# A weave of two matmul streams made eight units longer, with six transposes moved into it

## The chip, the cores and the metric

The kernel runs on one core of a Trainium2 chip. The metric is the device time of one execution in microseconds. The median of three runs before the change is 2181.49 us (2178.9 to 2183.92). The profile is of one more execution, of 2180.43 us.

## The reference

One layer of a streaming encoder on 256 rows of 2048 columns, all in 32-bit floating point. What matters here is the middle part, the mixer, with two branches whose results are merged by gates:

```
proj = x @ w_in                      # q, k, v, o of the mLSTM; sq, sk, sv; gates ga, gb
y_m  = head_norm(mlstm(q, k, v)) * sigmoid(o)          # 256 x 1024
y_sb = stick_breaking(sq, sk, sv)                      # 256 x 1024
merged = sigmoid(ga) * (y_m @ w_up_m) + sigmoid(gb) * (y_sb @ w_up_sb)   # 256 x 2048
x = layer_norm(ALPHA * x + merged @ w_out)
```

Ahead of it and behind it stands a SwiGLU network of 5632 hidden columns with a layer norm, and at the end an embedding that is added through a gate.

## The kernel before

**Units.** All large products run as units. A unit is one tile of weights (256 rows by up to 512 columns) against one half (128 rows, `t` = 0 or 1) of the activations. Both sides are split in two parts, a rounded one (`hi`) and the rest (`lo`), so a unit is six matmuls (lines 1286 to 1288): hi by hi, hi by lo and lo by hi, for two blocks of 128 rows. A tile of weights comes by DMA from the SP queue (line 1207) as a raw page; ScalarE makes the `hi` part (line 1235) and VectorE the `lo` part (line 1239), in `split_one`. How many raw pages and split tiles are held ahead is given by the mode: `HELD` has (5, 6) for "mix", (6, 6) for "woven" and (8, 6) for "wide".

**Two kinds of streams.** `group` makes plain units: each tile is used for `t` = 0 and `t` = 1, and the two results grow in two PSUM accumulators. `both7` makes two blocks of columns with seven products instead of eight: 28 units, each with a tile of its own, after sums of weights on VectorE (line 361) and of accumulators (lines 397 and 403). Products 1 and 2 have one accumulator each at a time; products 5, 7, 6, 4 and 3 are interleaved and have five open together. When the seven are closed, `in_two` plans the two sigmoids of a pair of results `DELAY["sig"]` = 5.0 us later (line 240 by way of `activate`).

**The weave.** `weave(main, side)` puts the units of `side` between those of `main`, in proportion to columns: after each main unit as many side units as keep the two at the same fraction. In the mixer, `main` is the mLSTM values `v`, the stick-breaking columns `sb`, the two gates of group 0 (`branch`) and the up groups `ups(0)`, `ups(1)`, `ups(2)`: 176 units, sixteen of them of half width, so 168 in whole columns. An up group `g` is eight units with `w_up_m` on `ymT` (the mLSTM half) and eight with `w_up_sb` on `ysbT`. `side` is five `both7` of 28 units: values of the stick-breaking heads, output gates, and `pair(1)`, `pair(2)`, `pair(3)`, the two gates of groups 1 to 3. After the weave come the mode "mix", `bring_back`, which fetches the four parked blocks of the residual rows (line 272), then `ups(3)` and the product with `w_out`.

**The end of an up group.** `up_done(g, half)` runs when an accumulator is complete. It has the planner go on (`sched.until`) until the gate's sigmoid for this half is emitted, then VectorE multiplies the accumulator with the gate (line 1047) and, at the second half, adds the two halves (line 1049). `merge_turn(g, t)` turns the merged 128 x 512 block for the `w_out` product: `transposed` takes a PSUM bank, TensorE transposes four blocks (line 290), ScalarE casts (line 292), VectorE subtracts (line 297). For group 3 it is spawned `DELAY["mt"]` = 3.2 us after the addition; for groups 0 to 2 in one entry of the program behind the weave.

**What sets the order.** The order of instructions on every engine is the order in which this Python program emits them. Each entry of `program` is a unit, a mode or a function. A planner (`Sched`) has a clock that a whole unit moves on by 6 x 0.2161 us; generators are spawned with a delay and run when the clock has passed it. The instructions that they emit stand in each engine's queue at that place. After each unit `splits_due` emits splits, and with them additions of line 361, until six split tiles are held. PSUM has one pool of eight banks (`PSUM_BUFS`), which accumulators and transposes share, and SBUF one pool of 48 pages; a tile that takes a freed bank or page waits for the last access to it.

```
def misc(shape):
    return ps_pool.tile(shape, F32, name="ms", tag="ps")
...
        if u.start:
            u.acc["ps"] = ps_pool.tile([P, COL], F32, name="mm", tag="ps")
```

Of the kernel before, what the change touches and what calls it, by code (L numbers as in the profile page):

```python
# [15 lines left out]
TT = S // P  # L16
# [160 lines left out]
def flat(pairs):  # L177
    return [u for p in pairs for u in p]
# [7 lines left out]
def kernel(  # L186
# [19 lines left out]
    sched = Sched()  # L206
# [19 lines left out]
    def act_tile():  # L226
        return page_pool.tile([P, 2, 4, P], F32R, name="actT", tag="page")
# [59 lines left out]
    def transposed(src, act, c, t):  # L287
        ps = misc([P, 4, P])
        for k in range(4):
            nc.tensor.transpose(ps[:, k], src[:, k * P:(k + 1) * P], ident[:])  # L290
        dst = act.get(c, t)
        nc.scalar.copy(dst[:, 0], ps[:])  # L292
        if act.soon:
            if c not in act.whole:
                act.whole[c] = big()
            nc.scalar.copy(act.whole[c][:, t * COL:(t + 1) * COL], ps.rearrange("q k s -> q (k s)"))  # L296
        nc.vector.tensor_tensor(out=dst[:, 1], in0=ps[:], in1=dst[:, 0], op=ALU.subtract)  # L297
        act.mark(c, t, 4)
        if act.soon and all(act.ready(c, h) for h in range(TT)):
            sched.spawn(form_turn(act, c), DELAY["form"] + 5.0 * c)  # L300
# [35 lines left out]
    def group(w, rows, col0, cols, act, done):  # L336

        accs = [{} for _ in range(TT)]
        pairs = []
        for i, r in enumerate(rows):  # L340
            tile = plain(rows_of(w, r, col0, cols))
            pairs.append([Unit(tile, t, accs[t], act, r // COL, r % COL // P,
                               i == 0, i == len(rows) - 1, done) for t in range(TT)])
        return pairs
# [88 lines left out]
    program = []  # L433

    def mode(name):
        program.append(Mode(name))
# [252 lines left out]
    def sb_columns(ps, t, heads):  # L689

        n = len(heads) * DS
        stage = temp()
        nc.scalar.copy(stage[:, :n], ps[:, :n])
        sched.spaced(sb_turn(t, stage, heads), DELAY["sbt"], BANK_GAP)
# [110 lines left out]
    def v_done(g):  # L805
        def done(ps, t):
            st["v", t, g] = big()[:, 0:2 * (DM + 1)].rearrange("q (h d) -> q h d", d=DM + 1)
            nc.scalar.copy(st["v", t, g][:, :, DM:], ones[:, 0:2].rearrange("q (h d) -> q h d", d=1))
            nc.scalar.copy(st["v", t, g][:, :, 0:DM], ps.rearrange("q (h d) -> q h d", d=DM))
            flags.add(("v", t, g))  # L810
        return done
# [38 lines left out]
    def ym_rows(c, t):  # L850
        r = (c * TT + t) * P
        return ym_away[r:r + P, :].rearrange("p (k a q) -> p k a q", k=2, a=4)
# [6 lines left out]
    def bring_ym_back(units):  # L859

        def one(c, t):
            ymT.tiles[c, t] = act_tile()
            nc.sync.dma_start(out=ymT.tiles[c, t][:].bitcast(F32), in_=ym_rows(c, t))

        out = []
        for i in range(0, len(units), 4):
            out += [lambda i=i: one(i // 8, i // 4 % 2)] + units[i:i + 4] if i < 16 else units[i:i + 4]
        return out
# [58 lines left out]
    def gated(h):  # L927

        yield from wait(("hs", h), ("mo", 0, h // 2), ("mo", 1, h // 2))
        due = max(sched.now, st.get("gated", 0.0))  # L930
        st["gated"] = due + GATED_GAP
        yield due - sched.now
        hs = st["hs", h // 2][:, h % 2]
        for t in range(TT):
            nc.vector.tensor_tensor(out=hs[:, t], in0=hs[:, t], in1=st["mo", t][:, h * DM:(h + 1) * DM], op=ALU.mult)
        yield bank(DELAY["m4"])
        ps = misc([P, TT, 2, P])
        parts = []
        for t in range(TT):
            for b in range(2):  # L940
                nc.tensor.transpose(ps[:, t, b], hs[:, t, b * P:(b + 1) * P], ident[:])
                k = 2 * (h % 2) + b
                parts.append((ymT.get(h // 2, t)[:, :, k], ps[:, t, b], hs[:, t, b * P:(b + 1) * P],
                              st["cw"][:, 64 + 2 * h + b:65 + 2 * h + b]))
        for _, src, y, g in parts:
            activate(y, src, ACT.Copy, scale=g)
        for d, _, y, _ in parts:
            nc.scalar.copy(d[:, 0], y)
            nc.vector.tensor_tensor(out=d[:, 1], in0=y, in1=d[:, 0], op=ALU.subtract)
        for t in range(TT):  # L950
            ymT.mark(h // 2, t, 2)
            if ymT.ready(h // 2, t):
                sched.spawn(put_ym_away(h // 2, t), DELAY["away"])
# [44 lines left out]
    def in_sequence(gens):  # L998
        for g in gens:
            yield from g  # L1000
# [10 lines left out]
    def v(g):  # L1011
        return flat(group(w_in, range(0, D, 2 * P), 2048 + g * COL, COL, x1T, v_done(g)))

    def sb(*heads):
        col0 = [(sq0 + h * DS, 2 * DS) for h in heads[::2]]
        return flat(group(w_in, range(0, D, 2 * P), col0, len(heads) * DS, x1T,
                          lambda ps, t: sb_columns(ps, t, heads)))
# [4 lines left out]
    def lane():  # L1022

        for h in heads:
            yield from stick(h)
# [6 lines left out]
    def gate_done(g, half):  # L1032
        def done(ps, t):
            if (g, t) not in gt:
                gt[g, t] = big()
            activate(gt[g, t][:, half * COL:(half + 1) * COL], ps, ACT.Sigmoid)
            flags.add(("gate", g, t, half))
        return done

    def merged(g, t):  # L1040
        return gt[g // 2 * 2, t][:, g % 2 * COL:(g % 2 + 1) * COL]

    def up_done(g, half, last):
        def done(ps, t):
            sched.until(lambda: ("gate", g, t, half) in flags)
            a = gt[g, t][:, half * COL:(half + 1) * COL]
            nc.vector.tensor_tensor(out=a, in0=ps, in1=a, op=ALU.mult)  # L1047
            if last:
                nc.vector.tensor_tensor(out=merged(g, t), in0=gt[g, t][:, 0:COL], in1=gt[g, t][:, COL:], op=ALU.add)
                if g == 3:  # L1050
                    sched.spawn(merge_turn(g, t), DELAY["mt"])
        return done

    def merge_turn(g, t):
        transposed(merged(g, t), mergedT, g, t)
        return
        yield

    def branch(g, half):
        return flat(group(w_in, range(0, D, 2 * P), ga0 + half * D + g * COL, COL, x1T, gate_done(g, half)))  # L1060

    def ups(g, swap=False):
        parts = [flat(group(w_up_m, range(0, HM * DM, 2 * P), g * COL, COL, ymT, up_done(g, 0, swap))),
                 flat(group(w_up_sb, range(0, HS * DS, 2 * P), g * COL, COL, ysbT, up_done(g, 1, not swap)))]
        if swap:
            parts.reverse()
        return parts[0] + parts[1]
# [10 lines left out]

    program.append(lambda: [sched.spawn(lane()) for _ in range(2)])
    program.append(lambda: sched.spawn(in_sequence([gated(h) for h in range(HM)])))  # L1080
    gate = branch(0, 1)
    main = v(0) + v(1) + sb(8, 9, 2, 3) + sb(10, 11, 4, 5) + [Mode("wide")] + sb(12, 13, 6, 7) + sb(14, 15) + [lambda: sched.spawn(lane())] + branch(0, 0) + gate[:4] + bring_ym_back(gate[4:] + ups(0)) + ups(1) + ups(2)
    mode("woven")
    program.extend(weave(main, both7(w_in, sq0 + 2 * HS * DS, sq0 + 2 * HS * DS + COL, x1T, sv_dest, sv_ready, 0)
                         + both7(w_in, 3072, 3072 + COL, x1T, mo_dest, mo_ready, 0) + pair(1) + pair(2) + pair(3)))
    mode("mix")
    program.append(bring_back)
    program.append(lambda: [sched.spawn(merge_turn(g, t), 1.0 + 2.0 * g + t) for g in range(3) for t in range(TT)])
    program.extend(ups(3))

    x2T = ActT(act_tile, ActT(act_tile))
    norm2 = Norm(ln2_g[0], ln2_b[0], x2T, ALPHA, (4.0, 1.0))
# [175 lines left out]
    for u in program:  # L1268
# [14 lines left out]
        for k in range(2):  # L1283
            hi, lo = a[:, 0, u.sub + k], a[:, 1, u.sub + k]
            first, last = u.start and k == 0, u.stop and k == 1
# [38 lines left out]
```

## Time and profile before

| | us |
|---|---|
| median of three runs (lowest, highest) | 2181.49 (2178.9, 2183.92) |
| the profiled execution's own time | 2180.43 |
| its span, first to last instruction | 2178.7 |
| TensorE busy with matmuls | 2170.4 |
| VectorE busy | 1936.1 |
| ScalarE busy | 1325.9 |
| first unit of the weave starts at | 806.16 |
| first unit behind the weave starts at | 1268.0 |

The span runs from the first to the last instruction; the execution's own time is 1.7 us longer. PE is TensorE's matmuls, PEld its loading of the stationary operand, DVE VectorE, ACT ScalarE, POOL GpSimd, SP the queue that issues nearly all DMAs. Matmuls overlap in the pipeline: one of 512 columns lasts about 0.39 us, but the next one starts 0.23 us after it, so time per unit is read from starts, and a busy TensorE says only that no gap was seen. The granted clock of TensorE is 1.00 in every stretch. In a row of a timeline stand start, duration, engine, line, operation, output and inputs, and in brackets the idle time of the engine before it with what ended it.

### The profile page before, as it was taken

To read this page: it belongs to the slowest core of one execution; us is meant where nothing else is said; L and a number is where in the kernel's file an instruction comes from. 1 tells how busy PE (TensorE), PEld (TensorE's weight loads), DVE (VectorE), ACT (ScalarE), POOL (GpSimd) and SP (SyncE) were. 2 spreads that over 40 slices of the span, in tenths; PEclk is the share of its full clock that TensorE was granted. 3 is DMA by queue.
4 is the path that set the end of the run, shared out by engine and by line. 5 is a ranking of instruction groups with operands and counts; after the bars stand their busy time and mean duration, and the time that the engine had idled before them with its cause. 6 is when DMAs were issued, how large, how long until landed. Compare 5 with 4: busy or idle time off the path is not lost.

```text
span 2178.7 us, 28297 instructions
## 1 busy us (share of the span) xinstructions
PE 2170.4 (100%) x9942; PEld 1796.9 (82%) x9942; DVE 1936.1 (89%) x2131; ACT 1325.9 (61%) x1632; POOL 97.9 (4%) x88
## 2 busy tenths in 40 slices
PE   9999999999999999999999999999999999999999
PEld 7888888888888888888888888888888888888888
DVE  6899999999998789898989985799999999999974
ACT  7565655556564766667766564565665555665572
POOL 0100000010000000000000000000010000000000
PEclk9999999999999999999999999999999999999999
DMA  9899999999995676776878876589999999999753
GB/s 328 254 300 287 288 291 309 282 278 314 313 326 174 212 229 210 224 232 202 281 233 270 283 263 211 183 235 312 286 279 302 296 284 291 311 297 319 259 165 101
DMA packets 304399, 572.72 MB, mean 263 GB/s; under 512 B 18392, under 2 KB 39808, under 8 KB 304256
## 3 DMA queue, kind: packets, MB, share of 16 engines
q1 hardware_dynamic: 282496, 528.96, 72.8%
q0 software_dynamic: 21760, 41.95, 11.2%
q8 instruction: 78, 1.28, 0.2%
q14 instruction: 65, 0.53, 0.1%
HBM read 564.55 MB, written 6.29 MB: 262 GB/s over the span
## 4 chain that ended last, share of the span: by engine, by line
PE 96%; DVE 2%; issue 1%; ACT 1%; DMA 0%; SPq 0%; DVEq 0%
PE mm L1286 31%; PE mm L1288 31%; PE mm L1287 31%; PE ms L290 1%; DVE split L1239 1%; DVE raw L361 1%; PE ms L496 0%; PE ms L987 0%; PE ms L885 0%; PE ms L963 0%; PE ms L900 0%; PE ms L976 0%; DVE temp L796 0%; ACT split L1235 0%; DMA big<-in_x_dram 0%
## 5 line engine op out<-in xcount | busy, mean ns | idle before, releaser
L1235 ACT CAST split<-raw 128x1024 fp32r<-128x1024 f32 (+2 forms) x1073 | 1072.5, 1038 | 535.6 <-PE mm L1287 170.9
L1239 DVE TENSOR_TENSOR split<-raw,split 128x1024 fp32r<-128x1024 f32 (+2 forms) x1073 | 1255.5, 1201 | 111.6 <-ACT split L1235 99.2
L1286 PE MATMUL mm<-split,actT 128*128 128x512 f32 (+2 forms) x3112 | 1214.0, 390 | 0.7 <-ACT big L240 0.4
L1288 PE MATMUL mm<-split,actT 128*128 128x512 f32 (+2 forms) x3112 | 1200.0, 386 | 0.6 <-DVE actT L297 0.6
L1287 PE MATMUL mm<-split,actT 128*128 128x512 f32 (+2 forms) x3112 | 1199.1, 385 | 0.4 <-DVE split L1239 0.3
L1288 PEld LDWEIGHTS mm<-split,actT 128*128 128x128 f32 x3112 | 584.7, 188 | 120.6 <-DVE actT L297 1.4
L1286 PEld LDWEIGHTS mm<-split,actT 128*128 128x128 f32 x3112 | 585.2, 188 | 115.9 <-DVE big L1047 1.2
L1287 PEld LDWEIGHTS mm<-split,actT 128*128 128x128 f32 x3112 | 585.5, 188 | 115.4 <-DVE split L1239 3.2
L361 DVE TENSOR_TENSOR raw<-raw 128x1024 f32<-128x1024 f32 x256 | 312.0, 1219 | 2.3
L1212 POOL DMA_DIRECT2D raw<-in_ffn_w_dram x80 | 95.5, 1193 | 1872.8 <-DMA raw<-in_ffn_w_dram 1150.8
L292 ACT CAST actT<-ms 128x512 fp32r<-128x512 f32 x60 | 35.1, 586 | 85.5 <-PE ms L290 84.8
L569 DVE TENSOR_TENSOR temp<-mm,temp 128x512 f32<-128x512 f32 x112 | 76.8, 685 | 3.5 <-PE mm L1288 1.2
L622 DVE SCALAR_TENSOR_TENSOR big<-mm,big 128x512 f32<-128x512 f32 x96 | 65.3, 682 | 3.5 <-PE mm L1288 3.5
L297 DVE TENSOR_TENSOR actT<-ms,actT 128x512 fp32r<-128x512 f32 x60 | 40.8, 684 | 19.3 <-ACT big L296 10.5
L285 DVE TENSOR_TENSOR actT<-temp,actT 128x512 fp32r<-128x512 f32 x40 | 26.5, 687 | 17.4 <-ACT actT L284 17.3
L236 ACT ACT_TABLE_LOAD x31 | 39.8, 1283 | 0.5
L240 ACT ACTIVATE temp<-mm 128x512 f32<-128x512 f32 (+1 forms) x22 | 12.3, 560 | 45.2 <-PE mm L1288 45.2
L240 ACT ACTIVATE temp<-temp 128x512 f32<-128x512 f32 (+1 forms) x48 | 28.6, 595 | 6.7 <-DVE temp L569 6.6
L284 ACT CAST actT<-temp 128x512 fp32r<-128x512 f32 x40 | 24.1, 621 | 13.0 <-DVE temp L308 12.0
L1098 DVE SCALAR_TENSOR_TENSOR big<-big,mm 128x512 f32<-128x512 f32 x8 | 5.5, 685 | 25.3 <-PE mm L1288 25.3
L240 ACT ACTIVATE temp<-ms,gbT 128x128 f32<-128x128 f32 x64 | 24.1, 460 | 5.6 <-PE ms L496 5.6
L1152 DVE TENSOR_TENSOR temp<-temp,big 128x512 f32<-128x512 f32 (+1 forms) x10 | 5.8, 582 | 23.7 <-ACT temp L240 23.7
(131 smaller groups left out, 562.5 us busy)
## 6 DMA issues: line engine op xcount, KB each, us to landing
raw<-in_ffn_w_dram SPq DMA_DIRECT2D x655, 512.0 KB, 6.0
raw<-in_w_in_dram SPq DMA_DIRECT2D x184, 512.0 KB, 4.6
raw<-in_ffn_w_dram POOLq DMA_DIRECT2D x80, 512.0 KB, 8.7
raw<-in_w_out_dram SPq DMA_DIRECT2D x32, 512.0 KB, 6.1
raw<-in_w_in_dram SPq DMA_DIRECT2D x56, 256.0 KB, 3.8
raw<-in_w_ple_gate_dram SPq DMA_DIRECT2D x24, 512.0 KB, 5.5
raw<-in_w_up_m_dram SPq DMA_DIRECT2D x16, 512.0 KB, 5.1
raw<-in_w_up_sb_dram SPq DMA_DIRECT2D x16, 512.0 KB, 5.5
```

What stands on the lines that cost most here:

```text
L236: nc.scalar.preload_act_table_set(table[0])
L240: nc.scalar.activation(out, in_, func, **kw)
L297: nc.vector.tensor_tensor(out=dst[:, 1], in0=ps[:], in1=dst[:, 0], op=ALU.subtract)
L361: nc.vector.tensor_tensor(out=out.tile[:, :, :cols], in0=a.tile[:, :, :cols], in1=b.tile[:, :, :cols], op=ALU.add)
L569: nc.vector.tensor_tensor(out=out, in0=a, in1=b, op=op)
L622: nc.vector.scalar_tensor_tensor(out=xs, in0=ps, scalar=0.5, in1=xs, op0=ALU.mult, op1=ALU.add)
L1212: nc.gpsimd.dma_start(out=r.tile[:, :, :r.cols], in_=r.plus[0], accum_op=ALU.add)
L1235: nc.scalar.copy(hi[:, ks], r[:, ks])
L1239: nc.vector.tensor_tensor(out=lo[:, ks], in0=r[:, ks], in1=hi[:, ks], op=ALU.subtract)
L1286: nc.tensor.matmul(ps, hi, w[0][:, k, :u.cols], start=first, stop=False)
L1287: nc.tensor.matmul(ps, hi, w[1][:, k, :u.cols], start=False, stop=False)
L1288: nc.tensor.matmul(ps, lo, w[0][:, k, :u.cols], start=False, stop=last)
```

## The change

`ups(3)` is made ahead of the weave and cut in two. Its first eight units (the mLSTM half) are appended to `main`, so the weave has 184 main units, 176 in whole columns, with the same 140 side units. Its second eight units stay behind the weave, after the mode "mix" and `bring_back`. The six `merge_turn` of groups 0 to 2 are spawned by a new entry `merge_turns` in `main`, between `ups(2)` and the eight units; their delays are 1, 4, 7, 10, 13 and 16 us instead of 1, 2, 3, 4, 5 and 6.

```diff
+    def merge_turns():
+        for g in range(3):
+            for t in range(TT):
+                sched.spawn(merge_turn(g, t), 1.0 + 3.0 * (2 * g + t))
+
+    gate, last = branch(0, 1), ups(3)
-    gate = branch(0, 1)
-    main = v(0) + v(1) + sb(8, 9, 2, 3) + sb(10, 11, 4, 5) + [Mode("wide")] + sb(12, 13, 6, 7) + sb(14, 15) + [lambda: sched.spawn(lane())] + branch(0, 0) + gate[:4] + bring_ym_back(gate[4:] + ups(0)) + ups(1) + ups(2)
+    main = v(0) + v(1) + sb(8, 9, 2, 3) + sb(10, 11, 4, 5) + [Mode("wide")] + sb(12, 13, 6, 7) + sb(14, 15) + [lambda: sched.spawn(lane())] + branch(0, 0) + gate[:4] + bring_ym_back(gate[4:] + ups(0)) + ups(1) + ups(2) + [merge_turns] + last[:8]
     mode("woven")
...
     mode("mix")
     program.append(bring_back)
-    program.append(lambda: [sched.spawn(merge_turn(g, t), 1.0 + 2.0 * g + t) for g in range(3) for t in range(TT)])
-    program.extend(ups(3))
+    program.extend(last[8:])
```

## The prediction

> **What bounds the kernel now.** I read the head of the page first, then the chain of waits, then a table of busy time by stage from the start of the weave, and last the engines' own timelines around the place of the edit.
>
> ```profile
> span 2178.7 us, 28297 instructions
> PE 2170.4 (100%) x9942; PEld 1796.9 (82%) x9942; DVE 1936.1 (89%) x2131; ACT 1325.9 (61%) x1632; POOL 97.9 (4%) x88
> PE 96%; DVE 2%; issue 1%; ACT 1%; DMA 0%; SPq 0%; DVEq 0%
> ```
>
> TensorE is never idle for long: 2178.7 - 2170.4 = 8.3 us in the whole span, and 96% of the chain that ended last is its matmuls. The edit takes no matmul and no transpose away. So it can win only time in which TensorE waits, and only near the place of the edit. The table by stage has that (columns: stretch, its length, busy time of PE, PEld, DVE, ACT, POOL, granted clock, DMA share, GB/s):
>
> ```profile
> 806.16:842.00 35.84, 35.54 (x161) 29.08 (x160) 33.72 (x46) 21.89 (x28) 0.00 (x0) 1.00 0.63 181
> 842.00:900.00 58.00, 57.87 (x255) 46.34 (x254) 55.26 (x64) 39.90 (x56) 0.00 (x0) 1.00 0.76 235
> ...
> 1100.00:1200.00 100.00, 99.28 (x441) 81.19 (x440) 87.50 (x93) 65.82 (x79) 0.00 (x0) 1.00 0.79 248
> 1200.00:1225.32 25.32, 25.32 (x114) 20.96 (x112) 25.25 (x24) 14.35 (x14) 0.00 (x0) 1.00 0.87 275
> 1225.32:1251.54 26.22, 26.03 (x114) 20.94 (x112) 26.12 (x27) 14.68 (x15) 0.00 (x0) 1.00 0.90 289
> 1251.54:1268.00 16.46, 16.46 (x73) 13.62 (x73) 16.39 (x17) 10.34 (x13) 0.00 (x0) 1.00 0.67 217
> 1268.00:1288.00 20.00, 20.00 (x101) 16.66 (x100) 19.93 (x25) 12.90 (x17) 0.00 (x0) 1.00 0.87 298
> 1288.00:1314.00 26.00, 26.00 (x120) 21.52 (x119) 13.60 (x15) 14.67 (x16) 0.00 (x0) 1.00 0.78 248
> sum 507.84, PE 506.47 PEld 416.80 DVE 458.17 ACT 338.81 POOL 0.00; mean PE 50.65 PEld 41.68 DVE 45.82 ACT 33.88 POOL 0.00
> ```
>
> The stretch 806.16 to 1268.00 is the weave, found by counting units of six matmuls in TensorE's order. Over it and the 46 us behind it TensorE idles 507.84 - 506.47 = 1.37 us. That is the whole stock of visible waits that the edit can reach. VectorE tells the other half: from 1200 to 1288 it is busy 87.69 of 88.00 us. It is full there, TensorE is just held. From 1288 on it has slack (13.60 of 26 us). Where VectorE does hold TensorE is seen in the waits of 1200 to 1315 and in the chain:
>
> ```profile
> PEld mm L1286 <- DVE big L1047: 0.6, 1, 0.6
> PEld mm L1287 <- DVE split L1239: 0.3, 1, 0.3
> ...
> 1250.89 0.61 DVE big L1047
> 1251.54 0.50 PE mm L1286
> ```
>
> At 1251.54 the first matmul of a new accumulator waits until VectorE has emptied an older one (line 1047): there is no free PSUM bank. The pool has eight (`PSUM_BUFS`); late in a pair of columns `both7` keeps five accumulators open, the up group two, and when one half group follows another two more are asked for.
>
> **The change part by part.** A unit takes 1.36 us, a group of four transposes about 0.47 us more than none, and a split on VectorE 1.15 us back to back:
>
> ```profile
> 1279.63 0.39 PE L1286 MATMUL mm<-split,actT 128*128 128x512 f32 x1
> 1280.99 0.39 PE L1286 MATMUL mm<-split,actT 128*128 128x512 f32 x1
> 1277.10 0.60 PE L290 MATMUL ms<-ident,big 128*128 128x128 f32 x4
> 1278.93 0.40 PE L1286 MATMUL mm<-split,actT 128*128 128x512 f32 x1
> 1256.54 6.89 DVE L1239 TENSOR_TENSOR split<-raw,split 128x1024 fp32r<-128x1024 f32 x6
> ```
>
> (1280.99 - 1279.63 = 1.36; 1278.93 - 1277.10 = 1.83 holds four transposes and one unit, so 0.47; 6.89 / 6 = 1.15.)
>
> *Eight units move into the weave.* Matmuls are the same in number: 0 on TensorE. What moves is VectorE's share. The main list grows from 168 to 176 units (in whole columns), so per main unit 140 / 176 = 0.80 side units follow instead of 0.83. A side unit costs VectorE one split and on average 16/28 of an addition (line 361, as long as a split), 1.15 x 1.57 = 1.81 us for 1.36 us of TensorE: 0.45 us too much. The eight moved units cost it four splits and two multiplications (line 1047, 0.68 us), 6.0 us for 10.9 us of TensorE: 4.9 us of VectorE's time come back inside the weave. The gain on the path is between 0 and the 1.37 us above; the waits lie at several places (806 to 842 has 0.30, 1100 to 1200 has 0.72, 1225 to 1251 has 0.19) and only the last and part of the rest feel a density that falls by 4.5%. I take 0.4 us.
>
> *Six merges move into the weave and apart.* Each is four transposes, a cast on ScalarE (line 292) and a subtraction on VectorE (line 297). TensorE's part is the same as before, six times 0.47 us; before, two of them stood together (0.89 instead of 0.94), so +0.05 us. What is new is where their PSUM bank comes from. Before, they came when all side accumulators were closed. Now five side banks and two up banks are open, so one bank is left, and each merge waits until VectorE has done the one before it. How long that takes, the six of before show:
>
> ```profile
> 1269.36 0.60 PE L290 MATMUL ms<-ident,big 128*128 128x128 f32 x4
> 1271.18 0.60 PE L290 MATMUL ms<-ident,big 128*128 128x128 f32 x4
> 1273.02 0.60 PE L290 MATMUL ms<-ident,big 128*128 128x128 f32 x4
> 1274.85 1.03 PE L290 MATMUL ms<-ident,big 128*128 128x128 f32 x8
> 1275.52 1.28 DVE L297 TENSOR_TENSOR actT<-ms,actT 128x512 fp32r<-128x512 f32 x2
> 1277.85 1.88 DVE L297 TENSOR_TENSOR actT<-ms,actT 128x512 fp32r<-128x512 f32 x3
> 1280.78 0.68 DVE L297 TENSOR_TENSOR actT<-ms,actT 128x512 fp32r<-128x512 f32 x1
> 1295.28 0.60 PE L290 MATMUL ms<-ident,big 128*128 128x128 f32 x4
> 1296.53 0.69 DVE L297 TENSOR_TENSOR actT<-ms,actT 128x512 fp32r<-128x512 f32 x1 [1.23 <-ACT actT L292]
> 1263.36 1.41 DVE L397 TENSOR_TENSOR big<-mm,big 128x512 f32<-128x512 f32 x2
> ```
>
> From the first transpose to the end of the subtraction: 1276.2 - 1269.36 = 6.8 us, then 5.6, 5.5, 4.3, 4.4, and 4.4 for the last (1277.10 to 1281.46); where VectorE was idle, 1.9 us (1295.28 to 1297.22). Before, nobody waited for these banks. In the change, writing out the order by the weave's rule and the planner's clock (1.297 us a unit), the merges follow after main unit 169, then 3, 2, 2 and 3 units later; the sixth is forced one unit later by the gate's wait below. In time: 3 x 1.36 + 0.47 = 4.5 us, or 2 x 1.36 + 0.47 = 3.2 us. Against turns of 6.8, 5.6 and 5.5 the second, third and fourth would wait 2.3, 2.4 and 2.3 us, 7.0 us in sum, if VectorE stayed as far behind as before. Two things speak for less. Each us that TensorE waits, VectorE catches up, so the waits don't add up: the sum tends to the largest, 2.4 us. And at the merges' start VectorE is less far behind: the side stands at 134 of 140, so six side units (6 x 0.45 = 2.7 us) and the closing sums of `both7` (lines 397 and 403, six of 0.68 us, 4.1 us) are backlog not yet made, and the first turn is near the idle one, 1.9 us. From there to the weave's end those 6.8 us come, the eight main units take 4.9 and six merges add 6 x (0.68 - 0.47) = 1.3: 3.2 us more, a turn of 5.1 us at the end and about 4.2 us at the fourth merge, which has 3.2: 1.0 us, once. The ends are 0 and 7.0; I take 1.0, since the full sum needs a backlog that doesn't shrink while TensorE stands.
>
> *Two gate waits move forward.* `up_done(3, 0)` needs the sigmoids of `pair(3)`, planned 5 us after their data. In the new order the stop of unit 175 comes 2.6 planned us after `rest` is queued, that of unit 176 only 1.3 us after the last side unit (m = 3), so `until` emits the sigmoids, and the sixth merge before them, at once. ScalarE then stands for VectorE's last subtraction, and behind it VectorE's multiplication stands for two sigmoids. The rows:
>
> ```profile
> 1267.25 0.63 ACT L240 ACTIVATE big<-big 128x512 f32<-128x512 f32 x1 [2.31 <-DVE big L403]
> 1274.13 1.15 ACT L240 ACTIVATE big<-big 128x512 f32<-128x512 f32 x2
> 1270.00 0.68 DVE L1047 TENSOR_TENSOR big<-mm,big 128x512 f32<-128x512 f32 x1
> 1291.39 0.69 DVE L1047 TENSOR_TENSOR big<-mm,big 128x512 f32<-128x512 f32 x1 [3.06 <-PE mm L1288]
> ```
>
> Two sigmoids are 1.15 us, so VectorE may stand 0 to 1.3 us. Queued behind that are splits for tiles up to six ahead, half a weave's tile time (1.9 us) or more each, so TensorE doesn't see it: 0, and 1.3 us if the six tiles of cover are used up by the backlog.
>
> *The eight units behind.* Only eight units now lie between the weave and the last merge. In before VectorE is back on time by 1288 (it idles 3.06 us before the row at 1291.39). Eight units take 10.9 us and ask 7.3 us of VectorE, so 3.6 us of backlog goes; 0.
>
> *The load of the parked rows* (`bring_back`, four transfers on SP) goes out behind eight more units' weights, closer to its first use:
>
> ```profile
> 1263.00 2.57 SPq L272 DMA_DIRECT2D big<-away x4
> DMA to landing us min/median/max: 3.3/8.3/9.7
> 1314.10 0.69 DVE L1098 SCALAR_TENSOR_TENSOR big<-big,mm 128x512 f32<-128x512 f32 x1 [7.90 <-PE mm L1288]
> ```
>
> It lands by 1276 and is used at 1314, 38 us later; with 10.9 us less, 27 us are left. 0. The four weights that go under the mode "wide" may have eight raw pages ahead instead of five, and six merged pages are taken while `x1T` is still in part alive; counted, about 40 of 48 pages are in use. 0; if pages ran short, loads would wait, and nothing here bounds that but the eight weights in hand.
>
> *The stick-breaking lanes* run on main units and meet 0.04 side units fewer per main unit, some 6 us by `ups(0)`. The last one's matmuls start at 1155.9, their first user comes at 1177.5: 0.
>
> Sum, against the profiled execution's own 2180.43 us: -0.4 + 0.05 + 1.0 = +0.65, 2181.1 us. The median of the three runs stands 1.06 us higher (2181.49), so I expect about 2182 us. With the bounds of the terms (-1.37 to 0, 0 to 7.0, 0 to 1.3) the median would lie between 2180 and 2190.
>
> **Rivals.** *Faster.* VectorE's full stretch is thinned and no bank is missed. All waits that the table has go: -1.37, 2180.1 us. For it speaks that the added units give VectorE 4.9 us; against a gain that counts, that 1.37 us is 0.06% of the time. To be faster by over 0.2% (4.4 us) half of all TensorE idle time of the span would have to go, most of which lies elsewhere. [...]
>
> *Slower: the one bank.* The merges wait as long as before's turns say, 2.3 + 2.4 + 2.3 = 7.0 us, 2189 us. The place is the six line 290 groups in the last 20 us of the weave, and it decides from a turn of about 5.5 us that holds through four merges. For it: VectorE is full, and 6 x 0.68 + 2 x 0.68 = 5.4 us come to it in that stretch. Against: TensorE's wait shortens the next turn. [...]
>
> *The merges aren't spread.* The gate's wait draws the sixth merge and the sigmoids forward and VectorE stands for ScalarE with the cover used up: 1.0 + 1.3, 2183.5 us. It ends within 0.2% all the same.
>
> **How the numbers follow.** 0.2% (4.4 us) is about what a measurement of this kernel can tell from no change. My forecast, with the rival of the drawn-forward merge, 0.77: 2182 us, own range 2179 to 2186. One bank, to its full price or half of it: 0.17, 2186 to 2190. Faster: a gain within 0.2% is in the forecast; beyond it 0.06, from something that no row shows. The range 2178 to 2188.5 leaves out about 0.06 below and a part of the slower case above.
>
> **What would show it.** Right: granted clock 1.00, VectorE full until the weave's end and with slack in the eight units behind it, line 290 groups four to six unit starts apart in the last 20 us of the weave, and one or two waits of TensorE for line 297 or 1047 of under 1.5 us each. TensorE's idle time over the weave stays between 0.5 and 3 us. Wrong: waits of over 2 us at three or more merges (the one bank); TensorE's queue standing for ScalarE's sigmoids or the splits behind them (line 1239) just after the weave; idle time before the first `w_out` evacuation at line 1098 from the parked rows; or a change of the idle time far ahead of the edit, where only the order of side and main units differs.

## The result, and the profile after

The changed kernel takes 2194.2 us (median of six runs, 2190.81 to 2196.77), the kernel before 2182.17 us in the same rounds: a ratio of 1.0053, 95% interval 1.0043 to 1.0064. It is slower by 0.5%, some 12 us. The forecast was 2182 us, no change. The profiled execution took 2190.81 us, the least of the six, so its profile, with a span 10.4 us longer than before, shows a little less than the median's loss.

The head of the page of the changed kernel, which answers to the first lines shown of before:

```profile
span 2189.1 us, 28303 instructions
PE 2171.9 (99%) x9942; PEld 1796.9 (82%) x9942; DVE 1937.2 (88%) x2131; ACT 1328.3 (61%) x1634; POOL 97.9 (4%) x88
PE 95%; DVE 3%; issue 1%; DMA 1%; ACT 1%; SPq 0%; DVEq 0%; ACTq 0%
```

No engine has more work: VectorE 1937.2 us against 1936.1, ScalarE 1328.3 against 1325.9 (two table loads more). TensorE's idle time grew from 8.3 to 17.2 us. The table of busy time by stage, from the start of the weave, finds it (columns as before: stretch, length, PE, PEld, DVE, ACT, POOL, granted clock, DMA share, GB/s):

```profile
...
900.00:1000.00 100.00, 100.00 (x457) 82.45 (x457) 89.09 (x117) 66.05 (x97) 0.00 (x0) 1.00 0.72 226
1000.00:1044.00 44.00, 44.00 (x238) 37.71 (x237) 33.48 (x47) 34.95 (x57) 0.00 (x0) 1.00 0.62 192
1044.00:1056.00 12.00, 8.84 (x54) 7.64 (x53) 12.00 (x19) 7.85 (x18) 0.00 (x0) 1.00 0.73 223
1056.00:1100.00 44.00, 44.00 (x205) 36.19 (x204) 41.95 (x53) 35.54 (x60) 0.00 (x0) 1.00 0.85 288
1100.00:1150.00 50.00, 50.00 (x225) 41.08 (x225) 37.90 (x45) 35.34 (x46) 0.00 (x0) 1.00 0.71 231
1150.00:1170.00 20.00, 18.23 (x80) 14.28 (x79) 19.88 (x21) 12.18 (x14) 0.00 (x0) 1.00 0.74 235
1170.00:1262.00 92.00, 92.00 (x407) 76.19 (x406) 88.50 (x87) 53.18 (x55) 0.00 (x0) 1.00 0.84 271
1262.00:1274.18 12.18, 8.39 (x40) 6.45 (x39) 12.11 (x14) 5.12 (x6) 0.00 (x0) 1.00 0.57 194
1274.18:1277.59 3.41, 3.41 (x9) 2.64 (x8) 2.77 (x3) 1.11 (x2) 0.00 (x0) 0.50 0.00 0
1277.59:1300.00 22.41, 22.41 (x108) 18.52 (x107) 19.00 (x22) 14.98 (x19) 0.00 (x0) 1.00 0.88 298
sum 494.50, PE 485.10 PEld 398.80 DVE 445.66 ACT 327.55 POOL 0.00; mean PE 40.42 PEld 33.23 DVE 37.14 ACT 27.30 POOL 0.00
```

TensorE idles 494.50 - 485.10 = 9.4 us in the twelve stretches, before 1.37. It is lost in few places: 3.16 us at 1044 to 1056, 1.77 at 1150 to 1170, 3.79 at 1262 to 1274. And for 3.41 us from 1274.18 the granted clock is 0.50, and matmuls of 512 columns start 0.43 us apart instead of 0.23: half of that time, an estimated 1.7 us, is lost to TensorE. The 8.0 us more of idle time and the 1.7 us are 9.7 of the 10.4 us. Who was waited for stands in the waits of 800 to 1310, of which these are TensorE's own:

```profile
PE ms L290 <- DVE actT L297: 2.4, 1, 2.4
PE mm L1290 <- DVE actT L993: 2.4, 1, 2.4
...
PE ms L290 <- DVE big L1047: 1.4, 1, 1.4
...
PE ms L987 <- DVE temp L845: 1.2, 1, 1.2
...
PE ms L987 <- ACT big L240: 0.8, 1, 0.8
...
PE mm L1290 <- ACT big L809: 0.6, 1, 0.6
...
PE mm L1290 <- DVE big L1047: 0.6, 1, 0.6
```

They add up to 9.4 us. The line numbers of the matmuls moved: L1290 to L1292 are L1286 to L1288 of before, L1243 and L1239 the splits. Only the rows of line 290 are the merges, at the end of the weave. The wait for line 993, the last step of a stick-breaking head, ends at 1053, 210 us ahead of the edit's place; those for 809, 240 and 845 lie ahead of it too (at 848, 1046 and 1154).

The engines' timelines at the merges show the waits of line 290:

```profile
1265.81 0.66 PE L290 MATMUL ms<-ident,big 128*128 128x128 f32 x4 [1.37 <-DVE big L1047]
1273.00 0.66 PE L290 MATMUL ms<-ident,big 128*128 128x128 f32 x4 [2.42 <-DVE actT L297]
1277.84 0.60 PE L290 MATMUL ms<-ident,big 128*128 128x128 f32 x4
...
1266.40 0.68 DVE L1047 TENSOR_TENSOR big<-mm,big 128x512 f32<-128x512 f32 x1
1267.11 0.69 DVE L1049 TENSOR_TENSOR big<-big 128x512 f32<-128x512 f32 x1
1267.72 1.22 DVE L361 TENSOR_TENSOR raw<-raw 128x1024 f32<-128x1024 f32 x1
1268.86 1.22 DVE L1243 TENSOR_TENSOR split<-raw,split 128x1024 fp32r<-128x1024 f32 x1
1269.99 1.22 DVE L361 TENSOR_TENSOR raw<-raw 128x1024 f32<-128x1024 f32 x1
1271.13 1.22 DVE L1243 TENSOR_TENSOR split<-raw,split 128x1024 fp32r<-128x1024 f32 x1
1272.26 0.68 DVE L297 TENSOR_TENSOR actT<-ms,actT 128x512 fp32r<-128x512 f32 x1
1272.86 2.35 DVE L1243 TENSOR_TENSOR split<-raw,split 128x1024 fp32r<-128x1024 f32 x2
1275.13 0.68 DVE L297 TENSOR_TENSOR actT<-ms,actT 128x512 fp32r<-128x512 f32 x1
```

The first merge's bank is held from 1265.81 to the end of line 297 at 1272.94, 7.1 us, since a multiplication with the gate, an addition of two halves, two additions of weights and two splits stand ahead of its subtraction in VectorE's queue. The second merge stands at 1270.6 and waits 2.42 us for that bank. The turns behind it are 1.9 to 3.7 us, and nobody waits again: while TensorE stood and then ran at half clock, VectorE caught up (before the third subtraction, at 1279.10, it is idle for 2.15 us).

### The profile page after: what moved, and what is told of

The parts are those of the page before. It is cut to its first block, busy times and chain, and to the rows that moved or that the text cites. A ratio compares the mean times of both kernels' runs of the same rounds, so it can differ in the third digit from the quotient of the medians.

```text
span 2189.1 us, 28303 instructions
## 1 busy us (share of the span) xinstructions
PE 2171.9 (99%) x9942; PEld 1796.9 (82%) x9942; DVE 1937.2 (88%) x2131; ACT 1328.3 (61%) x1634; POOL 97.9 (4%) x88
## 4 chain that ended last, share of the span: by engine, by line
PE 95%; DVE 3%; issue 1%; DMA 1%; ACT 1%; SPq 0%; DVEq 0%; ACTq 0%
PE mm L1290 30%; PE mm L1292 30%; PE mm L1291 30%; PE ms L290 1%; DVE split L1243 1%; DVE raw L361 1%; DMA raw<-in_ffn_w_dram 1%; PE ms L496 0%; ACT split L1239 0%; PE ms L987 0%; PE ms L885 0%; PE ms L963 0%; PE ms L900 0%; PE ms L976 0%; DVE temp L796 0%
## 5 line engine op out<-in xcount | busy, mean ns | idle before, releaser
L1239 ACT CAST split<-raw 128x1024 fp32r<-128x1024 f32 (+2 forms) x1073 | 1072.6, 1038 | 540.5 <-PE mm L1291 163.7
L1243 DVE TENSOR_TENSOR split<-raw,split 128x1024 fp32r<-128x1024 f32 (+2 forms) x1073 | 1257.7, 1203 | 122.1 <-ACT split L1239 102.5
L1290 PE MATMUL mm<-split,actT 128*128 128x512 f32 (+2 forms) x3112 | 1214.3, 390 | 3.6 <-DVE actT L993 2.4
L1292 PE MATMUL mm<-split,actT 128*128 128x512 f32 (+2 forms) x3112 | 1200.0, 386 | 0.6 <-DVE actT L297 0.6
L1292 PEld LDWEIGHTS mm<-split,actT 128*128 128x128 f32 x3112 | 584.9, 188 | 120.5 <-DVE actT L297 1.4
L1290 PEld LDWEIGHTS mm<-split,actT 128*128 128x128 f32 x3112 | 585.2, 188 | 117.8 <-issue 3.6
L285 DVE TENSOR_TENSOR actT<-temp,actT 128x512 fp32r<-128x512 f32 x40 | 26.5, 688 | 17.3 <-ACT actT L284 17.2
```

Of the source, the lines that this page charges most:

```text
L1239: nc.scalar.copy(hi[:, ks], r[:, ks])
L1243: nc.vector.tensor_tensor(out=lo[:, ks], in0=r[:, ks], in1=hi[:, ks], op=ALU.subtract)
L1290: nc.tensor.matmul(ps, hi, w[0][:, k, :u.cols], start=first, stop=False)
L1292: nc.tensor.matmul(ps, lo, w[0][:, k, :u.cols], start=False, stop=last)
```

## The experiments

Three theories stood at the start. A: there are two places, the front of the weave, where each side unit now stands a little later against the main units, and the merges at the end. B: the late half group, with its gate waits drawn forward, costs the time. C: the merges alone cost it. Ratios are to the kernel before, timed in the same rounds.

**The units alone** (`e1_units_only`): the changed kernel with the merges put back.

```diff
-    ... + ups(1) + ups(2) + [merge_turns] + last[:8]
+    ... + ups(1) + ups(2) + last[:8]
...
     program.append(bring_back)
+    program.append(lambda: [sched.spawn(merge_turn(g, t), 1.0 + 2.0 * g + t) for g in range(3) for t in range(TT)])
     program.extend(last[8:])
```

> The eight units stay in the weave, the six merges go back behind it with their old delays. Theory A (two places): the changed kernel loses about 4.5 us at 1045 to 1170 because all side units stand a little later against the main units, and about 6 us at 1264 to 1278 where merges wait for a bank; here the first stays and the second goes, +4 to +6 us over the kernel before. Theory B (the late half group itself, with its gate waits drawn forward, costs the time): +10 to +12 us stays. Theory C (the merges alone): within 2 us of the kernel before.

2187.81 against 2182.69 us, 1.0021 (1.0012 to 1.0030): +5.1 us, with no merge in the weave. Its waits in the front are those of the changed kernel, to 0.01 us (2.39 us for line 993, ending at 1055.74), and none of over 0.4 us stands at the end of the weave. Theory C falls, B's size too.

**The same front** (`e2_same_front`): the weave of before up to the first unit of `ups(1)`; the rest of the side units is woven with the rest of main, the eight units and the merges.

```diff
+    up1, up2 = ups(1), ups(2)
...
+    front = weave(main, side)                 # main ends with up1 + up2, as before
+    front = front[:front.index(up1[0])]
+    side = [u for u in side if u not in front]
...
+    program.extend(front)
+    program.extend(weave(up1 + up2 + [merge_turns] + last[:8], side))
```

> The weave is that of the kernel before up to the first unit of the second up group; only from there on the rest of the side units is spread over the rest of the main units with the eight units and the merges at its end. Theory A: the waits at 1045 to 1170 go back to those of before (0.9 us), the two waits of the merges and the clock's dip behind them stay, +5 to +7 us over the kernel before. Theory B and C: +10 to +12 us, as in the changed kernel.

2181.51 us, 0.9995 (0.9986 to 1.0004). All three theories missed: with the old front the whole edit costs nothing, merges in the weave included. Its timeline shows how the merges get by:

```profile
1261.17 0.60 PE L290 MATMUL ms<-ident,big 128*128 128x128 f32 x4
1266.39 0.60 PE L290 MATMUL ms<-ident,big 128*128 128x128 f32 x4
...
1259.18 0.68 DVE L1047 TENSOR_TENSOR big<-mm,big 128x512 f32<-128x512 f32 x1
1262.78 0.68 DVE L1047 TENSOR_TENSOR big<-mm,big 128x512 f32<-128x512 f32 x1
1265.23 0.68 DVE L297 TENSOR_TENSOR actT<-ms,actT 128x512 fp32r<-128x512 f32 x1
```

The first merge finds line 1047 done (1259.18) and turns in 4.7 us (1261.17 to 1265.91), and the second comes 5.2 us later and finds the bank free. The side units that the old front has done already are missing here, 26 over 40 main units from `ups(1)` on, so less stands ahead of the merge in VectorE's queue: behind the first transposes two splits, but one multiplication, one addition of halves and the rest of one addition of weights. That the thinner side does this was not tried apart from the rest of the edit.

**The same front, units alone** (`e3_same_front_units_only`): as the last, with the merges behind the weave as in e1.

> The old front and no merges in the weave: the eight units alone, at its end. Theory A: neither place loses, within 2 us of the kernel before, -1 us at best, since that is all the waiting there is. Theory B: the gate waits and the late units still cost, +5 us or more.

2181.14 us, 0.9994 (0.9986 to 1.0003). With the old front the late half group and its gate waits cost nothing; B falls. The possible gain of under 1 us can't be told from zero.

**A bank freed by ScalarE** (`e4_bank_freed_by_act`): the changed kernel, where the merges of groups 0 to 2 leave PSUM by a ScalarE copy.

```diff
-        transposed(merged(g, t), mergedT, g, t)
+        m, ps, dst = merged(g, t), misc([P, 4, P]), mergedT.get(g, t)
+        for k in range(4):
+            nc.tensor.transpose(ps[:, k], m[:, k * P:(k + 1) * P], ident[:])
+        nc.scalar.copy(m, ps.rearrange("q k s -> q (k s)"))
+        m = m.rearrange("q (k s) -> q k s", s=P)
+        split_psum(dst[:, 0], dst[:, 1], m)
```

> The changed kernel, but the merges of groups 0 to 2 copy their bank on ScalarE first, and VectorE subtracts from that copy, so the bank is free without VectorE (one more ScalarE copy of 0.6 us each). Theory A, with the bank behind VectorE's queue as the cause: the second wait of 2.4 us for line 297 falls below 1 us, the first (line 1047, 1.4 us) stays, the clock holds 1.00 there, and the time is 3 to 5 us under the changed kernel's. If VectorE's late splits hold TensorE and the bank only shows it: no change within 2 us.

2188.86 us, 1.0028 (1.0017 to 1.0039), where the changed kernel has 1.0053: some 5.5 us less, a little more than the 3 to 5 expected. The second wait and the half clock account for 2.4 + 1.7 us of it; the rest was not found. The first wait stays, the second is gone, and the clock holds (line 1060 is the transposes here):

```profile
1267.95 0.66 PE L1060 MATMUL ms<-ident,big 128*128 128x128 f32 x4 [1.36 <-DVE big L1047]
1272.55 0.60 PE L1060 MATMUL ms<-ident,big 128*128 128x128 f32 x4
1275.76 0.60 PE L1060 MATMUL ms<-ident,big 128*128 128x128 f32 x4
```

```profile
1262.00:1280.00 18.00, 16.64 (x82) 13.54 (x81) 17.93 (x20) 12.51 (x16) 0.00 (x0) 1.00 0.57 183
```

The merges have the same place in the order and VectorE is as full (17.93 of 18 us); what changed is who frees the bank. So the bank behind VectorE's queue is shown to be the cause of the second wait.

**Twice the distance** (`e5_spaced_6`): the delays 1.0 + 6.0 * (2 * g + t).

> The changed kernel with the merges 6 us apart instead of 3, so that three come in the weave and three behind it. If the second merge waits because the first one's subtraction stands 6 us deep in VectorE's queue: its wait of 2.4 us falls below 1 us and with it the dip, 3 to 5 us under the changed kernel, as e4. If each merge pays for itself: 1 to 2 us less.

2187.9 us, 1.0033 (1.0021 to 1.0046). The first merge stands 1.38 us for line 1047, the next comes 7.3 us after it and doesn't wait; no dip there, matmuls of 512 columns start 0.23 us apart. By the ratios that is some 4.4 us under the changed kernel, as expected.

**A stick's bank freed by ScalarE** (`e7_units_stick_by_act`): e1, and in the last step of `stick`

```diff
-        parts = [(ysbT.get(h // 4, t)[:, :, h % 4], ps[:, t * P:(t + 1) * P]) for t in range(TT)]
+        nc.scalar.copy(z[:, 0:S], ps[:])
+        parts = [(ysbT.get(h // 4, t)[:, :, h % 4], z[:, t * P:(t + 1) * P]) for t in range(TT)]
```

> As e1_units_only (5.1 us over the kernel before), but the last step of each stick-breaking head copies its bank on ScalarE first (one more ScalarE copy of 256 columns), and VectorE subtracts from that copy, so the bank is free without VectorE's queue. If the shifted front loses because the first gate's accumulator needs the bank that VectorE still holds (line 993): the wait of 2.4 us near 1050 falls below 1 us, the clock's dip behind it goes, 2 to 4 us under e1. If sticks are late for another reason: within 1 us of e1.

2183.86 us, 1.0011 (1.0002 to 1.0020), against 1.0021 of e1. These two intervals overlap, but the runs hardly do: e1's lie 2.7 to 6.4 us over the median of before, those of e7 0.5 to 4.1 us. The stretch around the wait in e1 and here:

```profile
1044.00:1055.64 11.64, 8.58 (x58) 7.60 (x56) 10.84 (x17) 10.04 (x22) 0.00 (x0) 1.00 0.80 259
1055.64:1059.06 3.42, 3.32 (x8) 2.69 (x9) 3.42 (x5) 0.00 (x0) 0.00 (x0) 0.50 0.75 192
```

```profile
1040.00:1060.00 20.00, 19.23 (x110) 16.80 (x110) 19.03 (x27) 15.11 (x30) 0.00 (x0) 1.00 0.91 297
```

In e1 TensorE loses 3.06 us, and the clock is 0.50 for 3.42 us; here it loses 0.77 us at a clock of 1.00. The timelines of the two main kernels say how the meeting comes about; of before, and then of the changed kernel:

```profile
1047.24 0.82 PE L987 MATMUL ms<-temp,big 128*128 128x256 f32 x4
1052.12 0.60 PE L941 MATMUL ms<-ident,big 128*128 128x128 f32 x4
...
1056.90 0.50 PE L1286 MATMUL mm<-split,actT 128*128 128x512 f32 x1
...
1050.03 0.48 DVE L993 TENSOR_TENSOR actT<-ms,actT 128x128 fp32r<-128x128 f32 x2
```

```profile
1042.05 0.60 PE L941 MATMUL ms<-ident,big 128*128 128x128 f32 x4
...
1046.21 0.92 PE L987 MATMUL ms<-temp,big 128*128 128x256 f32 x4 [0.76 <-ACT big L240]
...
1053.06 0.47 PE L1290 MATMUL mm<-split,actT 128*128 128x512 f32 x1 [2.40 <-DVE actT L993]
...
1052.43 0.48 DVE L993 TENSOR_TENSOR actT<-ms,actT 128x128 fp32r<-128x128 f32 x2
```

The sticks are planned in time, the first gate of `branch(0, 0)` by its place in main. With fewer side units per main unit that gate comes earlier: before, its first unit is at 1056.9, 9.7 us after the stick's matmuls; now it is due at 1050.6, 4.4 us after them, and VectorE empties that bank only at 1052.9. In between, the gated turn (line 941) and the stick (987) have changed their order. The bank is also held twice as long, 6.7 us from the stick's first matmul (1046.21 to 1052.91) against 3.3 us before (1047.24 to 1050.51); had it been held 3.3 us, the gate would not have waited.

**The front shifted without anything moved** (`e8_front_8`, `e9_front_16`, `e10_front_m8`): the kernel before; `weave` counts 8, 16 or -8 whole-width units too many up to `ups(1)`, and the rest makes up for it.

```diff
+    front = weave(main, side, 8 * COL)        # n = more + ...; 16 * COL; -8 * COL
+    front = front[:front.index(up1[0])]
...
+    program.extend(weave(up1 + up2, side))
```

> The kernel before with nothing moved; only up to the second up group the side units are spread as if main had eight units more, behind that they make up for it. If the shift of the front alone costs the time: +4 to +6 us, as e1. If it takes the moved units too: within 2 us of the kernel before.

> The same with sixteen units more, twice the shift. If a thinner side costs by itself: twice e8, +9 us or more. If the cost is a meeting of two bank users whose order and distance change with the shift: no such proportion; the place and size of the waits differ from e8, anything from 0 to +8 us.

> The same with eight units fewer, a denser side in front. If a thinner side costs by itself: 2 to 5 us under the kernel before. If it is a meeting of bank users: the first gate's accumulators come later than the stick's bank is freed, no wait of over 1 us there; within 2 us of the kernel before unless another meeting arises.

2189.07 us, 1.0032 (1.0020 to 1.0045); 2187.06 us, 1.0025 (1.0015 to 1.0036); 2182.41 us, 1.0001 (0.9992 to 1.0010). With 8 that is 7 us more, over the 4 to 6 expected: the same waits stand at the same places as in the front of the changed kernel, and more come in its denser end (1.1 us for line 1047, 0.8 us for a split). With 16 the wait for line 993 is 1.0 us, not twice as long, and the longest are in the denser end (1.9 and 0.8 us for line 1245, its splits). With -8, a denser side in front, no wait there is over 0.7 us and nothing is won. So the front's loss doesn't grow with the shift: it is a meeting of bank users, not the thinner side.

**Both banks** (`e12_both_by_act`, the changed kernel with e4's and e7's copies, and `e11_same_front_by_act`, e2 with both).

> The changed kernel with both banks freed by ScalarE: the merges' as in e4 and the sticks' as in e7. If the two waits of 2.6 us and the clock's dips behind them are the larger part of the loss: what stays is the waits of 0.9, 1.4, 0.8 and 1.5 us, +2 to +4 us over the kernel before. If something else in the changed kernel costs as well: +6 us or more.

> e2_same_front (old front, units and merges at the end) with both banks freed by ScalarE. If waiting for banks is all that is left to win: 0 to 1.5 us under the kernel before, which has 1.4 us of such waits. If the eight more ScalarE copies of the sticks and six of the merges cost: 0 to 2 us over it.

2184.31 us, 1.0014 (1.0005 to 1.0023), and 2181.48 us, 1.0001 (0.9992 to 1.0009). The two copies take about three quarters of the loss away (+2.8 us left of some 12). Freeing banks where nothing meets wins nothing.

**The merges apart, behind the weave** (`e6_before_apart`): the kernel before with delays 1.0 + 3.0 * (2 * g + t).

> The kernel before with the merges behind the weave 3 us apart (1 to 16 us) instead of 1 us. All theories: within 1.5 us of the kernel before, since nobody waits for these banks there.

2181.54 us, 1.0001 (0.9992 to 1.0010), as expected. No version beats the kernel before by more than the measurement shows.

## Why the prediction was wrong

**The reading of the bound held.** TensorE is the path, the edit can only add or remove its waits, and the stock to win was 1.37 us. e3, which takes what could be won, is within 0.1% of before. VectorE had slack sooner, as the sum said (22.66 of 25 us busy at 1200 to 1225, before full), and it won nothing.

**The step that failed first: "the stick-breaking lanes ... 0".** The prediction looked for a gain "only near the place of the edit", and named a change of idle time far ahead of it as its last sign of being wrong; that sign came. It saw that the front shifts by some 6 us and priced one distance, from the last head to its first user (21.6 us). It didn't ask which bank users the shift brings together on the way. That costs 5.1 us (e1), not quite half of the loss: the first gate's accumulator against a stick's bank, 2.4 us and, in e1's profile, 3.42 us at a clock of 0.50, and smaller waits of 0.8 and 1.2 us at two sticks (lines 240 and 845). The cause of the largest is shown by e7. Those of the smaller ones weren't tried.

**The second: "where their PSUM bank comes from", 1.0 us.** The mechanism was the right one, and the one-bank rival named its place. It measured 1.4 us for line 1047 and 2.4 us for line 297, and the half clock behind them 1.7 us. The size failed on the backlog: the prediction let the first turn start near the idle 1.9 us, because six side units were still to come; it measured 7.1 us. Splits and additions are emitted up to six tiles ahead of their use, so much of the last side units' work stood ahead of the merge already: the last addition of line 361 starts at 1269.99, ahead of the first subtraction, and splits and the closing sums alone come behind it. That waits don't add up, since VectorE catches up meanwhile, held: 2.42 us was the last of them. The rival's form was wrong, 7.0 us from three waits with a turn of about 5.5 us that holds: the turns were 7.1 and then 1.9 to 3.7 us. That the end came to 5.5 us, near the rival's price, is luck for the rival: 3.8 us were two waits, one of them for line 1047, and 1.7 us the clock.

**The clock.** The prediction put "granted clock 1.00" among the things that would show it right, and gave no chance to a dip. The changed kernel has two waits of 2.4 us on TensorE, one that ends at 1053 and one that ends at 1273; the rows around them:

```profile
1048.90:1052.31 3.41, 1.76 (x14) 1.52 (x12) 3.41 (x4) 2.49 (x6) 0.00 (x0) 1.00 0.81 252
1052.31:1055.73 3.42, 2.67 (x12) 2.22 (x13) 3.42 (x7) 0.41 (x2) 0.00 (x0) 1.00 0.65 209
1270.77:1274.18 3.41, 1.18 (x7) 1.06 (x8) 3.41 (x5) 1.47 (x2) 0.00 (x0) 1.00 0.03 10
1274.18:1277.59 3.41, 3.41 (x9) 2.64 (x8) 2.77 (x3) 1.11 (x2) 0.00 (x0) 0.50 0.00 0
```

Behind the first, of 2.40 us, the clock stays at 1.00. Behind the second, of 2.42 us, it is 0.50 for 3.41 us, from 1.2 us after the wait's end. In e1 it is 0.50 for 3.42 us from 1055.64, at the end of the wait of 2.39 us for line 993 (1055.74), the same wait that has no dip in the changed kernel. Without the waits it is 1.00 at these places: from 1040 to 1060 in e7, from 1262 to 1280 in e4. In the rows above TensorE idles 1.65 and 0.75 us at the first wait, and 2.23 us in the 3.41 us ahead of the dip. These cases don't settle what decides whether a dip stands behind a wait of 2.4 us.

What a dip costs is read from the half clock, an estimated 1.7 us (half of 3.41), and not from the times: the profiled execution of the changed kernel, with its one dip in these rows, has a mean clock of 0.999, and in e1 the three executions with 1.000 took 2186.8 to 2189.1 us, the eight with 0.999 2185.4 to 2188.8. The changed kernel's six go the other way, two with 0.999 at 2190.8 and 2191.7 us and four with 0.998 at 2194.1 to 2196.8; a second dip of 1.7 us would explain less than half of that gap. Nor does the mean tell the place: e7's profiled execution has 0.999 too.

**What was priced at nothing and cost nothing.** The gates drawn forward, eight units instead of sixteen behind the weave, the later load of the parked rows and the pages: e2 and e3 have all of these and are within 0.1% of before. Merges 3 us apart cost nothing as such either (e6).

**What stays open.** Some 0.7 us of the profiled difference lies outside the weave, and the median of the changed kernel lies 3.4 us over its profiled execution. e12 keeps 2.8 us, for which its waits (0.6, 0.8, 1.2, 0.6 and 1.4 us, less 1.4 of before's) are enough; they weren't taken apart.

## What to carry to other kernels

Where units are spread by proportion, making one list longer moves everything in front of the edit as well: keep the order ahead of the edit as it was and re-spread only what is behind it (e2 did just that, for the whole 12 us). When almost all PSUM banks are held, ask for each new user which engine frees the bank and what stands in that engine's queue as emitted, not as used; a copy by an engine with slack can free it sooner, as ScalarE's did in e4, where the wait of 2.4 us went. And a TensorE stall can cost more than its length: behind the one of 2.42 us the clock was 0.50 for 3.41 us.

## What the runs showed of the hardware

The granted clock of TensorE was 0.50 for 3.41 us from 1274.18 in the changed kernel, from 1.2 us after the end of a wait of 2.42 us, and for 3.42 us from 1055.64 in e1, at the end of a wait of 2.39 us. Matmuls of 512 columns started 0.43 us apart in these stretches and 0.23 us apart behind them. Behind the changed kernel's wait of 2.40 us, which ends at 1053.06, the clock stayed at 1.00.
